# A hybrid state-space, Fourier and attention step: adaLN in column groups between the x tiles, and a state output whose coefficient step is cut into parts

## The chip, the core and the metric

The kernel runs on one core of one Trainium2 chip. The metric is the device time of one execution in microseconds (us). The median of three runs of the kernel before is 2755.11 us (2753.56 to 2757.28).

TensorE is called PE here, VectorE DVE, ScalarE ACT, GpSimd POOL; SP is the engine whose queue issues nearly all DMAs.

## What is computed

Two layers work on 128 context tokens (conditioned by `c_ctx`) and 1024 latent tokens (by `c`), 1024 channels each. Cut to what matters here:

```python
m = silu(cvec) @ ada_w + ada_b
shift, scale, gate = split(m)
h = rmsnorm(x, norm_g) * (1.0 + scale) + shift
a_in, a_gate, f_in, f_gate, q, k, v, c_gate = split(h @ w_in)
for d in (forward, backward):
    a_bar, b_bar = s5_discretise(a_re[d], a_im[d], log_dt[d], b_re[d], b_im[d])
    hs = s5_scan(u32, a_bar, b_bar, h0, rev)
    y = y + real(einsum(hs, c_mat))
    finals.append(hs[:, 0] if rev else hs[:, -1])
za = gelu(ya) @ glu_w
yf = fourier_mix(f_in) @ fnet_w
yc = attention(rope(rms(q)), rope(rms(k)), v)
x = x + gate * (merge of the three gated branches) @ w_out
```

The outputs are both token sets after a final RMS norm, the context keys and values, and the final state of each scan direction.

## The kernel before, in words

Tokens stand along the free axis: channels on the 128 partitions, 1152 token columns in three thirds (`j`) of 384. Large products are made of three passes: each fp32 operand is split into a rounded high part and a low part (`whi`, `wlo`, `hh`, `hl`), and `mm3` issues three matmuls per 128 x 128 block of weights. `dense(n)` runs the next n blocks from a list: for each third, 8 channel blocks k, into a `pd` accumulator (two buffers), which ACT then evacuates into `jo` and SP stores.

The program is written as Python generators that `drive` interleaves by given rates. A scheduler then fixes the order of each engine's instructions when the program is built: it takes them by the order in which they were written, as soon as its own estimate says that they are ready. On the chip each engine's order is fixed, and semaphores hold an instruction until its inputs are there.

The change touches three places.

**The head** (`setup`, `ada_gen`, `ada_row`, `x_gen`, `rb_first_gen`, `h_first_gen`, and `run` at the end). Nine tiles of x (128 tokens each, 512 KB) are loaded, transposed on PE (`x_gen`, 8 transposes a tile, half of each evacuated by ACT and half by DVE at L415), and their squares summed. `ada_gen` computes the first layer's shift and scale: 16 weight units of 512 KB (`aw`, four buffers), two products of 512 columns a unit with the four columns of `silc` or `sc4` as stationary operand. Eight of the first 16 halves, and others, are split into `awr` (ACT rounds, DVE or POOL subtracts). A finished part is copied (`adarow`) and turned by four small matmuls with `sel`. `h_unit` then makes `hh` and `hl` for one k and one third: a multiply on DVE (L149 or L461), ACT with the bias, a subtraction on DVE. All x tiles come first, then the adaLN units.

**The final states** (`scan_gen`, `finals`). The scan is 128 steps of four DVE instructions on the states `H` (the tile `A1`, `A` in the profile). The context states end in column 16 after the sixteenth step. `finals`, called where the scan's generator ends, copies that column on ACT (`ss_fin`), transposes it twice on PE and stores it.

**The state output** (`ssm_out_gen`), after the q, k, v work of each layer and beside six dense blocks. For each of eight steps of four groups, `coef` multiplies exponents and output weights (`CA`: DVE product, POOL product, DVE sum, for real and imaginary part) and copies them into `CK` (L758 to L760, DVE). `toeplitz` multiplies `CK` on PE in four column groups (`tile_position`), and its result goes through DRAM into `TT` and on ACT into `TP`. Two steps later, four groups g are put out: three DVE copies (L803 to L805) turn the states of g into `Hg` (two buffers), then three products on PE and a GELU on ACT into `Y`, which is stored after every second step.

Helpers: L127 is every SP transfer, L142 every ACT instruction, L145 `tensor_tensor`, L149 `scalar_tensor_tensor`, L168 every matmul and L173 every transpose.

Of the kernel before, what the change touches and what calls it, by code (L numbers as in the profile page):

```python
# [18 lines left out]
DEPTH = 2  # L19
# [66 lines left out]
PACE = (1, 1)  # L86
HELD = 2
# [14 lines left out]
class Program:  # L102
# [73 lines left out]
    def setup(self):  # L176
# [3 lines left out]
        self.load_x(0, 1)  # L180
        self.identr = self.sb("identr", [128, 128], R)
        nc.gpsimd.dma_start(self.identr, I["ident"])
# [3 lines left out]
        for i in range(4):  # L186
            nc.vector.tensor_copy(self.fold[32 * i:32 * i + 32], self.ident[32 * i:32 * i + 32, 32 * i:32 * i + 32])
        self.half9 = self.sb("half", [128, 9])
        nc.gpsimd.memset(self.half9, -0.5)
        self.half = self.half9[:, :8]  # L190
        vecs = [("c", I["c"][0], 8), ("c_ctx", I["c_ctx"], 8), ("norm_g", I["norm_g"], 16), ("ada_b", I["ada_b"], 48),
                ("merge_b", I["merge_b"], 48)]
        st = self.sb("fvst", [128, 128], pool=self.xp)
        off = 0
        self.fv = {}
        col = self.sb("fv", [128, 128])
        for nm, ap, k in vecs:
            self.dma(st[off:off + k], ap.rearrange("l (k p) -> (l k) p" if len(ap.shape) == 2 else "(k p) -> k p", p=128))
            n = k // DEPTH
            for l in range(1 if len(ap.shape) == 1 else DEPTH):  # L200
                self.fv[nm, l] = col[:, off + n * l:off + n * l + (n if len(ap.shape) == 2 else k)]
            off += k
        ps = self.pst("pv")
        self.tr(ps[:, :off], st[:off])
        self.act(col[:, :off], ps[:, :off])
        self.mods = {}
        self.sel = self.sb("sel", [4, 2])
        self.dma(self.sel, I["sel"])
        self.silc = self.sb("silc", [128, KD, 4])
        nc.gpsimd.memset(self.silc, 0.0)  # L210
        sc = self.silc[:, :, 0:2]
        self.act(sc[:, :, 0], self.fv["c_ctx", 0], AF.Silu)
        self.act(sc[:, :, 1], self.fv["c", 0], AF.Silu)
        self.sc4 = self.sb("sc4", [128, KD, 4], R)
        self.act(self.sc4[:, :, 0:2], sc)
        self.tt(self.sc4[:, :, 2:4], sc, self.sc4[:, :, 0:2].bitcast(F), OP.subtract)
# [6 lines left out]
        self.dma(self.dmask, I["dmask"])  # L223
# [82 lines left out]
    def ada_gen(self, l, pool, parts, bufs=3, first=False):  # L306
        self.ada_alloc(l)
        units = [(o, k) for o in parts for k in range(4)]
        ld = {}
        def load(i):  # L310
            ld[i] = self.ada_load(l, pool, bufs, *units[i])
        for i in range(bufs - 1):
            load(i)
        for i, (o, k) in enumerate(units):
            if i + bufs - 1 < len(units):
                load(i + bufs - 1)
            if i == 0:
                pa = self.ps.tile([128, 3, 512], F, name="pa", tag="pa", bufs=1)
            ps = pa[:, i // 4 % 3]
            st = ld.pop(i)  # L320
            for h in range(2):
                ends = (k == 0 and h == 0, k == 3 and h == 1)
                if first and (h == 0 or i >= 16):
                    self.mm(ps[0:4, :], self.silc[:, 2 * k + h], st[:, h], *ends)
                else:
                    w = self.sb("awr", [128, 2, 512], R, bufs=3 if first else 2, pool=pool)
                    self.act(w[:, 0], st[:, h])
                    self.tt(w[:, 1], st[:, h], w[:, 0].bitcast(F), OP.subtract, e=self.nc.gpsimd if first and i >= 7 else None)
                    self.mm(ps[0:4, :], self.sc4[:, 2 * k + h], w[:, 0], ends[0], False)
                    self.mm(ps[0:4, :], self.sc4[:, 2 * k + h], w[:, 1], False, ends[1])  # L330
                if h == 0:
                    if i > 3 and k == 0:
                        self.ada_row(l, units[i - 1][0], row)
                    yield 2 * 216
# [3 lines left out]
            if i + 1 == len(units):  # L338
                self.ada_row(l, o, row)
            yield 2 * 216  # L340

    def ada_row(self, l, o, row):
        pc = self.pst("pt")
        for b in range(4):
            self.mm(pc[:, 2 * b:2 * b + 2], row[:, 128 * b:128 * b + 128], self.sel)
        self.ada_out(l, o, pc)
# [133 lines left out]
    def rb_first_gen(self, xT, ssq):  # L480
        self.tt(ssq[:, 0], ssq[:, 0], ssq[:, 1], OP.add)
        r = self.rstd_cols(ssq[:, 0], 9)
        self.rb = [self.rstd_rows(r[:, 3 * j:3 * j + 3], 3) for j in range(3)]
        self.h_tiles()
        self.xr0 = self.sb("xr0", [128, KD, 384], pool=self.xp)
        for k in range(KD):
            self.tt(self.xr0[:, k], xT[:, k, 0:384], self.rb[0], OP.mult)
            yield 500

    def h_first_gen(self, xT, js, ks):  # L490
        for j in js:
            for k in ks:
                if j == 0:
                    self.h_unit(0, j, k, self.xr0[:, k], None, self.xr_tile())
                else:
                    self.h_unit(0, j, k, xT[:, k, 384 * j:384 * j + 384], self.rb[j], self.xr_tile())
                yield 500
# [208 lines left out]
    def scan_gen(self, l):  # L706
# [31 lines left out]
    def ssm_out_gen(self, l, a_d, y_d):  # L738
# [8 lines left out]
        ca, tp = {}, {}  # L747
        U = {}

        def coef(i):  # L750
            g0 = 4 * i
            CA = self.sb("ss_CA", [128, 2, 4, 16, 8], bufs=3, pool=self.gp)
            y = self.outer(Er, Cr, Ei, Cn, g0, CA[:, 0])
            self.tt(CA[:, 0], CA[:, 0], y, OP.add)
            y = self.outer(Er, Cn, Ei, Cr, g0, CA[:, 1])
            self.tt(CA[:, 1], CA[:, 1], y, OP.subtract)
            for r, C in ((0, Cr), (1, Cn)):
                nc.vector.tensor_copy(CK[0:64, r, :, 8:15], CA[0:64, r, :, :, 0:7].rearrange("p q c t -> p q t c"))  # L758
                nc.vector.tensor_copy(CK[64:128, r, :, 0:7], CA[64:128, r, :, :, 1:8].rearrange("p q c t -> p q t c"))  # L759
                nc.vector.tensor_copy(CK[:, r, :, 7], C[:, g0:g0 + 4])  # L760
            ca[i] = CA

        def toeplitz(i):
            g0 = 4 * i
            ps = self.pst("pt")
            Bf = S["B"].rearrange("p g r c -> p (g r c)")
            for r in range(2):
                for q in range(4):
                    c0 = (g0 + q) * 32 + 16 * r
# [13 lines left out]

        for x in range(10):
            if 1 <= x < 9:
                toeplitz(x - 1)
            if x < 8:
                if x % 2 == 0:
                    U[x // 2] = self.u_load(a_d, x // 2)
                coef(x)  # L790
            yield 2000 if x == 0 else 1200
            i = x - 2
            if i < 0:
                continue
            g0 = 4 * i
            if i % 2 == 0:
                Y = self.sb("ss_Y", [128, 8, 145], bufs=1, pool=self.gp)
            for q in range(4):
# [796 lines left out]
```

## Time and profile before

| what | us |
|---|---|
| median of three runs | 2755.11 |
| the profiled execution's own time | 2752.03 |
| its span | 2750.3 |
| PE busy (16092 matmuls) | 2627.0 |
| DVE busy | 1826.6 |
| ACT busy | 1143.5 |
| POOL busy | 683.4 |

The span is the time from the first to the last recorded instruction of one execution; the own time of that execution is 1.7 us longer. Busy time is the sum of an engine's instructions. A matmul's end is modelled, so a busy PE can still run at a lower clock: PEclk is the share of full speed that was granted, 1.00 for 2.4 GHz and 0.50 for 1.2 GHz. A wait is put down to the engine and line that released it.

### The profile page before, as it was taken

To read this page: it belongs to the slowest core of one execution; us is meant where nothing else is said; L and a number is where in the kernel's file an instruction comes from. 1 tells how busy PE (TensorE), PEld (TensorE's weight loads), DVE (VectorE), ACT (ScalarE), POOL (GpSimd) and SP (SyncE) were. 2 spreads that over 40 slices of the span, in tenths; PEclk is the share of its full clock that TensorE was granted. 3 is DMA by queue.
4 is the path that set the end of the run, shared out by engine and by line. 5 is a ranking of instruction groups with operands and counts; after the bars stand their busy time and mean duration, and the time that the engine had idled before them with its cause. 6 is when DMAs were issued, how large, how long until landed. Compare 5 with 4: busy or idle time off the path is not lost. (4 is left out here: it accounts for less than half of the span.)

```text
span 2750.3 us, 44553 instructions
## 1 busy us (share of the span) xinstructions
PE 2627.0 (96%) x16092; PEld 2509.0 (91%) x16092; DVE 1826.6 (66%) x3933; ACT 1143.5 (42%) x2676; POOL 683.4 (25%) x521
## 2 busy tenths in 40 slices
PE   7998999899999999999999899999999999999998
PEld 3898999799999999999989899989989998999998
DVE  6549955856558889866572797577654788891343
ACT  5461145331355565423345322543223655553244
POOL 3241122322321020132343212233222202102223
PEclk9999999999999999999999999999999999999999
DMA  6632223566263345544543222345645334433244
GB/s 223 178 99 84 95 87 110 150 191 207 86 202 114 110 138 153 173 126 114 165 146 93 95 89 84 107 125 160 211 154 174 109 121 150 143 121 98 80 121 149
DMA packets 459997, 366.85 MB, mean 133 GB/s; under 512 B 72953, under 2 KB 432001, under 8 KB 459777
## 3 DMA queue, kind: packets, MB, share of 16 engines
q1 hardware_dynamic: 458480, 359.75, 42.9%
q0 software_dynamic: 1296, 4.26, 0.5%
q8 instruction: 127, 2.08, 0.3%
q14 instruction: 94, 0.76, 0.1%
HBM read 243.52 MB, written 120.39 MB: 132 GB/s over the span
## 5 line engine op out<-in xcount | busy, mean ns | idle before, releaser
L168 PE MATMUL pd<-hh,whi 128*128 128x384 f32 x2496 | 857.1, 344 | 24.0 <-ACT jo L142 20.1
L168 PE MATMUL pd<-hh,wlo 128*128 128x384 f32 x2496 | 844.6, 339 | 3.2 <-POOL wlo L145 3.2
L168 PE MATMUL pd<-hl,whi 128*128 128x384 f32 x2496 | 843.1, 338 | 1.3 <-DVE hl L149 1.3
L145 POOL TENSOR_TENSOR wlo<-wst,whi 128x512 fp32r<-128x512 f32 x312 | 437.9, 1405 | 1525.8 <-ACT whi L142 1404.8
L168 PEld LDWEIGHTS pd<-hh,whi 128*128 128x128 f32 x2496 | 472.5, 189 | 35.0 <-ACT jo L142 22.8
L168 PEld LDWEIGHTS pd<-hh,wlo 128*128 128x128 f32 x2496 | 472.5, 189 | 7.8 <-POOL wlo L145 5.7
L168 PEld LDWEIGHTS pd<-hl,whi 128*128 128x128 f32 x2496 | 473.1, 190 | 3.8 <-DVE hl L149 2.3
L168 PE MATMUL pd<-A,whi 128*128 128x384 f32 x1728 | 458.2, 342 | 8.2 <-ACT jo L142 4.9
L168 PEld LDWEIGHTS pd<-A,whi 128*128 128x128 f32 x1728 | 311.2, 189 | 11.7 <-ACT jo L142 5.6
L142 ACT ACTIVATE whi<-wst 128x512 fp32r<-128x512 f32 x312 | 196.0, 630 | 278.5 <-PE pd L168 190.6
L168 PE MATMUL pd<-A,wlo 128*128 128x384 f32 x864 | 293.9, 340 | 0.0
L1078 DVE TENSOR_REDUCE at_mx<-pa 128x1 f32<-128x1152 f32 x128 | 173.3, 1354 | 16.1 <-PE pa L168 15.7
L168 PE MATMUL pa<-at_K,at_Q 128*128 128x384 f32 x768 | 167.2, 347 | 8.6 <-ACT at_P L142 5.8
L142 ACT ACTIVATE at_PT<-pt 128x384 fp32r<-128x384 f32 (+1 forms) x260 | 114.9, 490 | 144.0 <-PE pt L173 143.6
L142 ACT ACTIVATE at_P<-pa,at_mx 128x1152 f32<-128x1152 f32 x128 | 158.1, 1235 | 20.7 <-DVE at_mx L1078 19.4
L168 PEld LDWEIGHTS pd<-A,wlo 128*128 128x128 f32 x864 | 163.2, 189 | 0.1
L168 PEld LDWEIGHTS pa<-at_K,at_Q 128*128 128x128 f32 x768 | 128.3, 188 | 29.0 <-ACT at_P L142 25.5
L168 PE MATMUL pt<-qkW,hh 128*128 128x384 f32 x576 | 150.7, 343 | 0.0
L168 PE MATMUL pv<-at_PT,at_V 128*128 128x256 f32 x1152 | 148.8, 283 | 0.0
L168 PEld LDWEIGHTS pv<-at_PT,at_V 128*128 128x128 f32 x1152 | 144.7, 191 | 0.8
L142 ACT ACTIVATE jo<-pd 128x384 f32<-128x384 f32 x120 | 58.0, 485 | 198.1 <-PE pd L168 96.5
L145 DVE TENSOR_TENSOR at_PT<-pt,at_PT 128x384 fp32r<-128x384 f32 (+1 forms) x260 | 133.1, 550 | 10.0 <-ACT at_PT L142 7.8
(294 smaller groups left out, 3772.3 us busy)
## 6 DMA issues: line engine op xcount, KB each, us to landing
aw<-in_ada_w_dram SPq DMA_DIRECT2D x48, 512.0 KB, 4.8
wst<-in_merge_w_dram SPq DMA_DIRECT2D x96, 256.0 KB, 3.0
wst<-in_w_in_dram SPq DMA_DIRECT2D x80, 256.0 KB, 2.9
td<-jo SPq DMA_DIRECT2D x96, 192.0 KB, 2.3
jt<-td SPq DMA_DIRECT2D x96, 192.0 KB, 2.8
wst<-in_w_out_dram SPq DMA_DIRECT2D x64, 256.0 KB, 2.9
sgd<-jo SPq DMA_DIRECT2D x72, 192.0 KB, 2.0
jt<-sgd SPq DMA_DIRECT2D x64, 192.0 KB, 2.7
```

The lines of the kernel that those rows point to most:

```text
L142: return self.nc.scalar.activation(out, in_, func, **kw)
L145: return (e or self.nc.vector).tensor_tensor(out=out, in0=a, in1=b, op=op)
L168: return self.nc.tensor.matmul(out, w, x, start=first, stop=last, **kw)
L1078: nc.vector.tensor_reduce(out=mx[:, 0:1], in_=src, axis=AX.XY if m3 else AX.X, op=OP.max, negate=True)
```

## The change

In the head, the four parts of adaLN are computed in plain fp32, without `awr`. The conditioning columns stand in `silp`, padded with zeros to 32 columns, and the eight products of a part go to four groups of 32 columns of PE (`tile_position=(0, 32 * q)`); the sum over the groups is in the matmuls with `fold4`, which also turn the row. There are seven `aw` buffers in place of four. The parts stand between the x tiles: three tiles, part 2, a tile, part 0, two tiles, `h` of four k for two thirds, part 3, a tile, part 1, the rest. The RMS factors are made for each third by itself. Loads of x are spread between the `aw` loads; norm_g, ada_b, merge_b and dmask are loaded on POOL's queue; `sel` is no longer loaded.

`finals` is called after the q, k, v work, and its copy is on DVE, pinned behind DVE's instructions written before it.

In the state output, the coefficient step is a generator of four parts that alternate with the four groups put out. The `CK` copies are on ACT. `turned` makes `Hg` two groups ahead with three buffers (`HGB`).

```diff
-    def ada_gen(self, l, pool, parts, bufs=3, first=False):
+    def ada_first_gen(self, l, pool, parts):
...
+            if i % 4 == 3:
+                for t in ((3,), (4, 5), (6,), (7, 8))[i // 4]:
+                    self.load_x(t, t + 1)
...
             for h in range(2):
-                ends = (k == 0 and h == 0, k == 3 and h == 1)
-                if first and (h == 0 or i >= 16):
-                    self.mm(ps[0:4, :], self.silc[:, 2 * k + h], st[:, h], *ends)
-                else:
-                    w = self.sb("awr", [128, 2, 512], R, bufs=3 if first else 2, pool=pool)
-                    self.act(w[:, 0], st[:, h])
-                    self.tt(w[:, 1], st[:, h], w[:, 0].bitcast(F), OP.subtract, e=self.nc.gpsimd if first and i >= 7 else None)
-                    self.mm(ps[0:4, :], self.sc4[:, 2 * k + h], w[:, 0], ends[0], False)
-                    self.mm(ps[0:4, :], self.sc4[:, 2 * k + h], w[:, 1], False, ends[1])
...
+                q = 2 * (k % 2) + h
+                self.mm(ps[32 * q:32 * q + 32], self.silp[:, 2 * k + h], st[:, h], k < 2, k >= 2, tile_position=(0, 32 * q))
+            if i + bufs < len(units):
+                load(i + bufs)
             if k == 3:
-                row = self.sb("adarow", [4, 512], bufs=1, pool=pool)
-                self.act(row, ps[0:4, :])
...
+                row = self.sb("adarow", [128, 512], bufs=1, pool=pool)
+                self.act(row, ps)
+                pc = self.pst("pv")
+                for b in range(4):
+                    self.mm(pc[:, 2 * b:2 * b + 2], row[:, 128 * b:128 * b + 128], self.fold4)
...
+    def rb_first(self, ssq, j):
+        c = slice(3 * j, 3 * j + 3)
+        self.tt(ssq[:, 0, c], ssq[:, 0, c], ssq[:, 1, c], OP.add)
+        self.rb[j] = self.rstd_rows(self.rstd_cols(ssq[:, 0, c], 3), 3)
...
-        self.finals(l)
...
-        self.act(fin, H[:, :, :, 16])
+        self.tc.keep_in_program_order(self.nc.vector.tensor_copy(fin, H[:, :, :, 16]))
...
+        def coef_gen(i):
...
+            for r, (a, b, op) in enumerate(((Cr, Cn, OP.add), (Cn, Cr, OP.subtract))):
+                y = self.sb("ss_o2", [128, 4, 16, 8], bufs=1, pool=self.gp)
+                self.tt(CA[:, r], e4(Er), f4(a), OP.mult)
+                self.tt(y, e4(Ei), f4(b), OP.mult, e=nc.gpsimd)
+                self.act(CK[:, r, :, 7], a[:, g])
+                yield
+                self.tt(CA[:, r], CA[:, r], y, op)
+                self.act(CK[0:64, r, :, 8:15], CA[0:64, r, :, :, 0:7].rearrange("p q c t -> p q t c"))
+                self.act(CK[64:128, r, :, 0:7], CA[64:128, r, :, :, 1:8].rearrange("p q c t -> p q t c"))
+                if r == 0:
+                    yield
...
+        def turned(g):
+            t = self.sb("ss_Hg", [128, 2, 145], bufs=HGB, pool=self.gp)
...
+            cg = coef_gen(x) if x < 8 else iter(())
+            og = out_gen(x - 2) if x >= 2 else iter(())
             for q in range(4):
...
+                next(og, None)
+                next(cg, None)
+                yield (3 * 246 if x >= 2 else 500) + (600 if q == 0 else 0)
...
                     drive((q, 78), (self.dense(2), 21))
+                    self.finals(l)
...
+            self.run_some(xg, 6)
+            self.h_tiles((0,))
+            self.rb_first(ssq, 0)
+            for k in range(KD):
+                self.xr_first(xT, k)
             next(ada)
+            self.run_some(xg, 2)
+            next(ada)
+            self.run_some(xg, 4)
+            self.h_tiles((1,))
+            self.rb_first(ssq, 1)
+            for j in range(2):
+                for k in range(4):
+                    self.h_first(xT, j, k)
+            next(ada)
+            self.run_some(xg, 2)
+            next(ada)
+            for k in range(4, 8):
+                self.h_first(xT, 0, k)
+            self.run_all(xg)
+            self.run_all(ada)
+            self.h_tiles((2,))
+            self.rb_first(ssq, 2)
+            for k in range(4, 8):
+                self.h_first(xT, 1, k)
+            for k in range(KD):
+                self.h_first(xT, 2, k)
```

## Rows read from the trace of the kernel before

**Rows 1.** The page, busy time of PE to POOL over the span.

```profile
PE 2627.0 (96%) x16092; PEld 2509.0 (91%) x16092; DVE 1826.6 (66%) x3933; ACT 1143.5 (42%) x2676; POOL 683.4 (25%) x521
```

**Rows 2.** Timeline of ACT, first layer's scan: start, duration, instruction, idle before.

```profile
223.66 0.32 ACT L142 ACTIVATE ss_fin<-A 128x64 f32<-128x64 f32 x1 [12.25 <-DVE A L145]
```

**Rows 3.** Timeline of PE at the same place of both layers.

```profile
224.93 0.69 PE L168 MATMUL pd<-hh,whi 128*128 128x384 f32 x1 [7.84 <-ACT jo L142]
...
1566.74 0.69 PE L168 MATMUL pd<-hh,whi 128*128 128x384 f32 x1 [7.83 <-ACT jo L142]
```

**Rows 4.** Windows, first stall: PE, PEld, DVE, ACT, POOL, PEclk, DMA share, GB/s.

```profile
225.00:230.00 5.00, 5.00 (x16) 5.00 (x17) 4.72 (x18) 0.26 (x1) 0.85 (x1) 0.50 0.40 131
...
240.00:250.00 10.00, 10.00 (x60) 10.00 (x59) 9.45 (x35) 2.63 (x5) 2.13 (x2) 1.00 0.16 54
```

**Rows 5.** Timeline of PE in the head.

```profile
24.50 1.02 PE L168 MATMUL pa<-aw,silc 128*4 128x512 f32 x2
...
65.16 0.34 PE L168 MATMUL pd<-hh,whi 128*128 128x384 f32 x1
...
81.79 0.44 PE L168 MATMUL pd<-hl,whi 128*128 128x384 f32 x1 [0.60 <-DVE hl L149]
```

**Rows 6.** Windows over the head, columns as in group 4.

```profile
8.40:36.50 28.10, 24.02 (x112) 12.78 (x113) 14.51 (x41) 19.63 (x42) 2.13 (x1) 1.00 0.87 317
36.50:82.30 45.80, 37.52 (x144) 19.12 (x143) 39.99 (x76) 25.57 (x53) 21.31 (x13) 0.85 0.62 207
```

**Rows 7.** Windows of 2.5 us in the head, columns as in group 4.

```profile
12.50:15.00 2.50, 2.33 (x12) 1.93 (x11) 1.41 (x5) 2.47 (x8) 0.00 (x0) 1.00 1.03 419
...
35.00:37.50 2.50, 2.50 (x14) 1.17 (x14) 1.04 (x3) 1.39 (x3) 0.00 (x0) 1.00 0.74 235
```

**Rows 8.** Waits of the SP queue, 0 to 70 us: total us, times, longest.

```profile
SPq L127 <- PE pa L168: 15.5, 11, 2.1
```

**Rows 9.** Waits of PE, state output of the first layer, 480 to 560 us.

```profile
PE pt L168 <- issue: 3.4, 1, 3.4
PE pa L168 <- DVE ss_Hg L805: 2.3, 1, 2.3
PE pt L168 <- DVE ss_CK L760: 1.9, 2, 1.3
```

**Rows 10.** Waits of PE, state output of the second layer, 1820 to 1960 us.

```profile
PE pa L168 <- DVE ss_Hg L805: 3.3, 3, 1.7
PE pt L168 <- issue: 2.4, 1, 2.4
PE pd L168 <- ACT jo L142: 1.9, 1, 1.9
```

**Rows 11.** Window of 20 us in the state output, columns as in group 4.

```profile
480.00:500.00 20.00, 14.72 (x90) 11.06 (x89) 19.16 (x32) 6.52 (x15) 8.66 (x6) 0.83 0.62 171
```

**Rows 12.** Timeline of DVE behind the first layer's scan.

```profile
369.01 0.17 DVE L871 TENSOR_SCALAR qk_ss<-qk_ss 128x4 f32<-128x4 f32 x1 [10.85 <-ACT qk_j L142]
```

**Rows 13.** Timeline of PE at a Toeplitz step.

```profile
510.87 1.02 PE L168 MATMUL pt<-ss_CK,ss_B 128*32 128x240 f32 x16
511.82 0.44 PE L168 MATMUL pd<-hh,whi 128*128 128x384 f32 x1
```

**Rows 14.** Groups of instructions, 0 to 85 us: count, busy us, mean ns.

```profile
L149 DVE SCALAR_TENSOR_TENSOR xr<-A,modA,rb 128x384 f32<-128x384 f32 x16 | 12.6, 800 | 0.0
...
L145 DVE TENSOR_TENSOR xr<-A,rb 128x384 f32<-128x384 f32 x8 | 8.2, 1090 | 1.5 <-ACT rb L142 1.5
...
L145 DVE TENSOR_TENSOR awr<-aw,awr 128x512 fp32r<-128x512 f32 x7 | 4.6, 687 | 2.6 <-ACT awr L142 2.6
```

**Rows 15.** Instructions that read modA, 0 to 85 us: ns min/median/max.

```profile
L149 DVE SCALAR_TENSOR_TENSOR xr<-A,modA,rb x16: 604/608/1648, 49.0 to 79.6; 128x384 f32<-128x384 f32 x16
```

**Rows 16.** Instructions on ss_CK, whole span: ns min/median/max.

```profile
L758 DVE COPY ss_CK<-ss_CA x32: 549/1027/1490, 485.4 to 1912.7; 64x448 f32<-64x448 f32 x32
```

**Rows 17.** Instructions on ss_TP, whole span: ns min/median/max.

```profile
L142 ACT ACTIVATE ss_TP<-ss_TT x16: 1078/1104/1122, 504.8 to 1933.9; 128x512 f32<-128x512 f32 x16
```

More of the change, by code (lines that the diff above doesn't have):

```diff
@@ L86 @@
 PACE = (1, 1)
+HGB = 3
 HELD = 2
@@ L187, in setup @@
             nc.vector.tensor_copy(self.fold[32 * i:32 * i + 32], self.ident[32 * i:32 * i + 32, 32 * i:32 * i + 32])
+        self.fold4 = self.sb("fold4", [128, 2], pool=self.xp)
+        nc.vector.tensor_reduce(self.fold4, self.ident.rearrange("p (q c) -> p c q", c=32)[:, 0:2], axis=AX.X, op=OP.add)
         self.half9 = self.sb("half", [128, 9])
@@ L190, in setup @@
         self.half = self.half9[:, :8]
[L191 to L194, printed above, removed]
         self.fv = {}
[L196 to L202, printed above, removed]
@@ new lines, in setup @@
+        for i, vs in enumerate(vecs):
+            n = sum(k for _, _, k in vs)
+            st = self.sb(f"fvst{i}", [n, 128], pool=self.xp)
+            col = self.sb(f"fv{i}", [128, n])
+            off = 0
+            for nm, ap, k in vs:
+                (pdma if i else self.dma)(st[off:off + k], ap.rearrange("l (k p) -> (l k) p" if len(ap.shape) == 2 else "(k p) -> k p", p=128))
+                m = k // DEPTH
+                for l in range(1 if len(ap.shape) == 1 else DEPTH):
+                    self.fv[nm, l] = col[:, off + m * l:off + m * l + (m if len(ap.shape) == 2 else k)]
+                off += k
+            ps = self.pst("pv")
+            self.tr(ps[:, :n], st)
+            self.act(col, ps[:, :n])
+            if i == 0:
+                self.load_x(0, 3)
@@ L304, in ada_load @@
         return st
-    def ada_gen(self, l, pool, parts, bufs=3, first=False):
+    def ada_first_gen(self, l, pool, parts):
         self.ada_alloc(l)
         units = [(o, k) for o in parts for k in range(4)]
-        ld = {}
+        bufs, ld = 7, {}
         def load(i):
             ld[i] = self.ada_load(l, pool, bufs, *units[i])
-        for i in range(bufs - 1):
+            if i % 4 == 3:
+                for t in ((3,), (4, 5), (6,), (7, 8))[i // 4]:
+                    self.load_x(t, t + 1)
+        for i in range(bufs):
             load(i)
+        pa = self.ps.tile([128, 3, 512], F, name="pa", tag="pa", bufs=1)
         for i, (o, k) in enumerate(units):
[L315 to L318, printed above, removed]
             ps = pa[:, i // 4 % 3]
@@ L478, in h_gen, with xr_first, h_first @@
                 yield 900
[L480 to L497, printed above, removed]
+    def rb_first(self, ssq, j):
+        c = slice(3 * j, 3 * j + 3)
+        self.tt(ssq[:, 0, c], ssq[:, 0, c], ssq[:, 1, c], OP.add)
+        self.rb[j] = self.rstd_rows(self.rstd_cols(ssq[:, 0, c], 3), 3)
+    def xr_first(self, xT, k):
+        self.tt(self.xr0[:, k], xT[:, k, 0:384], self.rb[0], OP.mult)
+    def h_first(self, xT, j, k):
+        if j == 0:
+            self.h_unit(0, j, k, self.xr0[:, k], None, self.xr_tile())
+        else:
+            self.h_unit(0, j, k, xT[:, k, 384 * j:384 * j + 384], self.rb[j], self.xr_tile())
     def rhs_h(self, k, j):
```

135 lines of the change are left out of this document (54 added, 81 removed).

## The prediction, made before the changed kernel was run

> **What bounds the kernel now.** The page first [rows 1]: TensorE (PE) is busy 2627 of 2750 us, so only PE's idle time, some 123 us, and time at its lower clock can be won; work moved between other engines counts only where PE waits for it. I then took PE's waits one by one and looked at the three places that the diff touches.
>
> *The final states.* Inside the first layer's scan, ACT stands still for 12.25 us in front of one 0.32 us copy, `ss_fin<-A`, that waits for DVE [rows 2]: column 16 of the states is written by the sixteenth scan step, and ACT has the copy ahead of the evacuation of PE's accumulators. PE runs on for a while on its two `pd` buffers and then idles 7.84 us for `jo`, and 7.83 us at the same place of the second layer [rows 3]. It comes back at 0.50 of its clock, the 1.2 GHz level: 16 matmuls in 5 us against 60 in 10 later [rows 4], (30-16)/30*5 = 2.3 us more. So each layer pays about 10.2 us.
>
> *The head.* The first dense matmul starts at 65.16 us, but PE still waits for `hl` at 81.79 [rows 5]; that is a late piece of the last third of the first block, so the dense stage is in full flow only from about 82. What DVE does up to there: 14.5 us busy of the first 28.1, then 40.0 of 45.8 [rows 6]. DVE is the bound of the second half because the first was half empty: the adaLN units come late. Loads ran at 419 GB/s while x came in and at 235 around 35 us [rows 7], when the SP queue waited eleven times, 15.5 us in all, for PE to free a weight buffer [rows 8].
>
> *The state output.* PE waits in the stage around 480 to 560 us for the Toeplitz coefficients (3.4 and 1.9) and for the turned states (2.3) [rows 9]; in the second layer for turned states 3.3, Toeplitz 2.4 and smaller ones [rows 10]. In 480 to 500 us DVE is busy 19.16 of 20, ACT only 6.52, and the mean clock is 0.83 [rows 11].
>
> **The change, part by part.**
>
> *Final states: -20 us.* The copy goes from ACT to DVE, behind everything issued there before it, and the call moves from the end of the scan to the end of the q, k, v work. Nothing then holds ACT in the scan, so 2*10.2 = 20.4 us go. Does another thing catch PE 10 us later? Behind the scan DVE idles 10.85 us until ACT has evacuated the first `qkv` product [rows 12], so the scan is not what PE would meet next: that slack takes up the 10.2 us nearly whole. What is added: one DVE copy of about 0.3 us (ACT's 0.32), the same two transposes, two ACT copies and one store, now at the pool's end. Nothing queues behind a long wait, but the next pool's tiles in the same memory may start later by that chain. The nearest row for a step of it is the 0.32 us copy, so five short steps and a store are bounded by 0 and about 3 us a layer; I take 0.2, since six dense blocks are there to cover it. -20.
>
> *Head: -18 us.* Removed: seven DVE subtractions `awr`, 4.6 us, and nine on GpSimd; 16 ACT roundings; half the adaLN matmul forms. All 32 products are now plain fp32, two PE instructions each, 1.02 us a pair [rows 5]: 33 us if serial. They go to four column groups. The nearest row for that is the Toeplitz step: sixteen instructions of 240 columns in 1.02 us, next full matmul 0.95 us after their start [rows 13]; so groups overlap, and two at a time I cost the units at 16*1.02 = 16 us, spread over a head in which PE has room. Each switch of shape shows as 0.1 us there (0.44 for 0.34), times 32 is 3 us, off the path; I take 0.
>
> The Trainium skill, TensorEngine Tiling (Array Packing), Key Properties, says that changing the tiling mode, not just the tile, drains TensorE, and here x transposes at full width alternate with the groups. By that rule, were no overlap left, PE would have 16 us more to do in the head, and my term would shrink to about -8; the row above shows a cost of a tenth of a microsecond instead, so the trace does not bear out the dear reading.
>
> Loads: x and 16 adaLN units are 25 transfers of 512 KB, 13.1 MB. At 419 GB/s that is 31 us, at 235 it is 56 [rows 7]. Buffers go from four to seven and PE frees them without a rounding chain in between, so I take near the upper rate: last unit at about 40 us. DVE: 54.5 us of work [rows 6] less 4.6 for `awr`; 16 products `xr` took 0.80 us in the mean for 0.608 in the median, 3.1 us, and eight others took 1.09 for 384 columns where `awr` took 0.687 for 512, so at least 3.2 [rows 14, 15]; GpSimd ran its subtractions beside them and has none now. About 43.5 us are left; they start when the first x tile lands, at 8.4 us now (where the first window begins [rows 6]), hence 52 us if DVE never waits. Three rms chains (GpSimd power, transposes, ACT) and four adaLN rows come in between: an estimate of 10 us of waiting, of the 19 us there now [rows 6]. So the last `hl` is ready at about 62 instead of 82: -20, and PE, which idles more just before, starts a few microseconds at its lower clock: +2.3 as after the stalls above. -18. Ends: -24 (few waits) and -8 (loads at 235 GB/s: 56 us and then the last 12 pieces of `h`, about 1.2 us each, to 72, plus 2). What is moved: x loads of the SP queue now stand between adaLN loads, five small loads go to the GpSimd queue (nothing there waits but the first power), three short powers replace one; all lie beside the loads of the first 10 us.
>
> *State output: -14 us.* Listed idle time is 3.4+2.3+1.9 in the first layer and 3.3+2.4 in the second, with small ones some 8 us each; the clock adds about (1-0.83)*20 = 3.4 us, part of it idle anyway, say 2. That is 20 us for both layers, and 5 more in waits at the end of the stage and the start of the next [rows 10]. The coefficient step's four copies leave DVE (about 1.03 us each for half of them [rows 16]), so some 25 us a layer go to ACT. ACT's nearest row is the permuted copy of 512 columns, 1.104 us [rows 17]: for 448 columns at most that, four a step, eight steps: 35 us a layer on an engine idle two thirds of the stage; costed at nothing, as long as ACT does not wait itself. Turned states are made two groups ahead with a third buffer, which takes away DVE's 2.3 and 3.3. Of the Toeplitz waits I keep half: the chain multiply, GpSimd, add, copy stays as long, only more dense work stands in front of its first use. So -14, between 0 and -24, with a loss bounded in the rivals.
>
> Sum: -20-18-14 = -52. Against the profiled execution (2752.03; its span 2750.3) that gives 2700; its time is 3 below the median of 2755.1, so **2703**.
>
> **Rivals.**
> 1. *The head stays bound by loads* (four waits for a buffer in PE's order): -8 instead of -18, 2713. For it: today's 235 GB/s. Against: 419 with the same transfers when nothing held them. 0.13.
> 2. *State output gains nothing*: PE's order is fixed when the program is built, and each Toeplitz step may again be placed before its coefficients. 2717. For it: the 3.4 us wait at such a place. 0.14.
> 3. *The final states' stall only moves*: PE's transposes or the next pool wait for the pinned copy. If half comes back, 2713. Against: DVE has slack behind the scan [rows 12]. 0.08.
> 4. *Slower: ACT's queue in the state output.* Each of 32 half steps puts two copies on ACT that wait for a DVE add, which waits for GpSimd; a `jo` evacuation queued behind them stops PE as in rows 2 and 3. PE covered 12.25-7.84 = 4.4 us there, so it decides from waits of over 4.4 us. The end is slower if all cost over (20+18)/32 = 1.2 us beyond that; at 1.6 each, 51 us, the time is 2768. Against: GpSimd's product is part of a 5 us chain already. 0.05.
> 5. *Column groups do not overlap* (the drain, told above): 2713. 0.06.
>
> **Numbers.** The main case has 0.54, own range 2690 to 2716. The rivals on the gaining side reach 2717, two of them together about 2727; below, head and state output both at their ends give 2687. Range 2687 to 2730. A measurement can tell about 0.2%, 5.5 us, from no change; only the fourth rival, or all the others together, gets there: faster 0.92, same 0.03, slower 0.05.
>
> **What would show it.** No ACT wait of 12 us in the scan, no 7.8 us PE wait, and a scan that ends at the same distance from its start. Last PE wait for `hl` near 62 us, adaLN loads over by 42, no `awr`. PE's waits for `ss_Hg` gone, for `ss_CK` halved, now put down to ACT. I am wrong if the scan's 10 us come back as a PE wait in the q, k, v stage, if the last `hl` is later than 72 us, or if PE's waits for `jo` grow in the state output.

## The result, and the profile after

The changed kernel takes **2717.83 us** (median of four runs, 2706.61 to 2720.30), against 2755.34 (median of four, 2753.56 to 2757.28): a ratio of 0.986, with a 95% interval of 0.984 to 0.988. The forecast was 2703, its range 2687 to 2730. The profiled execution took 2717.28 us with a span of 2715.5, 34.8 less than before, where the sum had -52.

The first part of the page, answering to [rows 1]:

```profile
span 2715.5 us, 44526 instructions
PE 2604.6 (96%) x16093; PEld 2504.5 (92%) x16093; DVE 1762.0 (65%) x3837; ACT 1201.1 (44%) x2754; POOL 669.1 (25%) x518
```

PE's busy time fell by 22.4 us and its idle time by 12.4. Busy time can fall although nearly the same matmuls run, because fewer of them run at the lower clock; that returns below. DVE lost 65 us, ACT gained 58: work moved between engines that do not set the end.

**A ruler.** To see where the 34.8 us came from, I counted the matmuls into `pd` (10,086 records in either trace). The n-th is the same piece of dense work in both, so its start is a clock on the work. Between two counts, the difference says what a stage gained:

| stage (n of the `pd` matmul) | before, us | after, us | gained |
|---|---|---|---|
| head (start to 288, four dense blocks) | 0 to 123.3 | 0 to 114.8 | 8.4 |
| first scan's stall (648 to 720) | 212.8 to 236.0 | 204.2 to 216.7 | 10.7 |
| first state output (1584 to 2376) | 474.5 to 668.9 | 454.8 to 644.5 | 4.7 |
| second scan's stall (5688 to 5760) | 1554.6 to 1577.6 | 1526.9 to 1539.3 | 10.5 |
| second state output (6624 to 7344) | 1816.6 to 1996.9 | 1777.6 to 1956.6 | 1.4 |
| everything else, to n = 10080 (4.6 gained between these stages, 5.7 lost behind the last) | | | -1.1 |

**The scan.** The windows of the first scan, answering to [rows 4] at the same place of the work (columns: window, its length, PE, PEld, DVE, ACT, POOL busy with instructions, granted clock, DMA share, GB/s):

```profile
215.00:220.00 5.00, 5.00 (x30) 5.00 (x30) 4.86 (x11) 1.36 (x3) 2.76 (x2) 1.00 0.29 92
220.00:225.00 5.00, 5.00 (x31) 5.00 (x30) 4.66 (x22) 0.49 (x1) 0.00 (x0) 1.00 0.29 92
```

No gap and no 0.50 behind it; the 7.84 and 7.83 us of [rows 3] are gone. The copy is now on DVE, some 240 us later in the first layer, and takes less than ACT's 0.32:

```profile
L716 DVE COPY ss_fin<-A x2: 205/207/209, 463.1 to 1785.5; 128x64 f32<-128x64 f32 x2
```

**The head.** PE's own sequence (columns: start, us, instructions, and in brackets the idle time before and its releaser), answering to [rows 5]:

```profile
10.62 0.48 PE L174 MATMUL pt<-ident,hl 128*128 128x128 f32 x1 [7.23 <-DMA hl<-in_x_prompt_dram]
...
24.63 1.92 PE L169 MATMUL pa<-aw,silp 128*32 128x512 f32 x16
...
42.45 3.63 PE L169 MATMUL pa<-aw,silp 128*32 128x512 f32 x16
46.86 1.05 PE L169 MATMUL pv<-fold,adarow 128*128 128x2 f32 x8 [0.79 <-ACT adarow L143]
...
51.70 1.97 PE L174 MATMUL pt<-ident,hl 128*128 128x128 f32 x8 [2.85 <-ACT A L143]
54.22 0.69 PE L169 MATMUL pd<-hh,whi 128*128 128x384 f32 x1 [0.55 <-ACT whi L143]
...
72.62 0.44 PE L169 MATMUL pd<-hl,whi 128*128 128x384 f32 x1 [0.64 <-DVE hl L150]
```

Read three things. Sixteen instructions of 512 columns run in 1.92 us: eight products at 0.24 us each, where one took 1.02 before [rows 5]. The last adaLN part is turned at 46.86, and the last x tile is transposed at 51.70, after it. The first dense matmul starts 11 us earlier (54.22 for 65.16), and the last wait for `hl` is at 72.62 instead of 81.79.

The windows show what the loads did, and what DVE did up to that last `hl`; the last two answer to [rows 6]:

```profile
5.00:10.00 5.00, 0.00 (x0) 0.00 (x0) 0.00 (x0) 0.00 (x0) 0.00 (x0) 1.00 1.04 178
30.00:35.00 5.00, 3.01 (x20) 1.47 (x24) 4.16 (x14) 4.11 (x12) 1.01 (x1) 1.00 1.04 397
40.00:45.00 5.00, 5.00 (x24) 2.72 (x27) 3.18 (x12) 0.90 (x3) 0.00 (x0) 0.50 1.12 337
45.00:50.00 5.00, 3.06 (x24) 1.75 (x16) 1.58 (x7) 2.44 (x7) 0.00 (x0) 0.84 0.17 26
10.60:48.00 37.40, 28.40 (x161) 16.27 (x162) 22.91 (x72) 20.01 (x43) 1.89 (x2) 0.91 0.98 348
48.00:72.60 24.60, 19.02 (x89) 17.55 (x87) 22.12 (x43) 15.82 (x33) 6.63 (x5) 0.72 0.46 169
```

The transfers are over by 45, and the DMA share is near or above 1 up to there. DVE has 14.5 us idle of the first 37.4 and is then busy 22.1 of 24.6. PE runs at 0.50 in 40 to 45 and at 0.72 in the mean of 48 to 72.6. What DVE waited for between its first x tile and 73 us (its four longest totals; 1.6 us more in two single waits):

```profile
DVE mod L146 <- PE pv L169: 6.4, 3, 3.8
DVE A L407 <- PE pt L174: 4.2, 5, 1.9
DVE hl L150 <- ACT hh L143: 2.3, 5, 0.6
DVE xr L146 <- ACT rb L143: 2.2, 1, 2.2
```

**The state output.** PE's waits in the first layer, over the whole stage of the ruler (455 to 645), answering to [rows 9]:

```profile
PE pd L169 <- ACT jo L143: 2.2, 1, 2.2
PE pa L169 <- ACT ss_TP L143: 2.0, 2, 1.8
PE pt L169 <- ACT ss_CK L143: 1.6, 2, 0.9
PE pd L169 <- DVE jo L150: 1.6, 3, 0.8
PE pt L169 <- issue: 1.3, 1, 1.3
PE pv L174 <- DVE ss_fin L716: 1.2, 1, 1.2
PE pd L169 <- POOL wlo L146: 1.1, 1, 1.1
```

[Rows 9] stop at 560 us. Over the whole stage before (474 to 669) they become these, with the Toeplitz waits as they were:

```profile
PE pa L168 <- DVE ss_Hg L805: 3.1, 2, 2.3
PE pd L168 <- ACT jo L142: 3.0, 1, 3.0
PE pd L168 <- DVE jo L149: 1.6, 2, 0.9
PE pa L168 <- ACT ss_TP L142: 1.0, 1, 1.0
```

In the second layer after (1777 to 1957), answering to [rows 10], and then two lines of the whole stage before (1816 to 1997) that stand beside those:

```profile
PE pd L169 <- ACT jo L143: 3.2, 2, 2.9
PE pd L169 <- DVE jo L150: 2.4, 4, 0.9
PE pa L169 <- ACT ss_TP L143: 2.2, 2, 1.4
PE pt L169 <- ACT ss_CK L143: 1.6, 2, 0.9
PE pt L169 <- issue: 1.3, 1, 1.3
```

```profile
PE pd L168 <- DVE jo L149: 1.6, 2, 0.9
PE pa L168 <- ACT ss_TP L142: 0.6, 1, 0.6
```

The turned states (`ss_Hg`) are gone from both lists, and the Toeplitz waits (issue and `ss_CK`) fell from 3.4 + 1.9 to 1.3 + 1.6 in the first layer. What stands there instead is mostly put down to ACT: `ss_TP`, `ss_CK`, `jo`. The waits for `jo`, ACT's and DVE's together, went from 4.6 to 3.8 in the first layer and from 3.5 to 5.6 in the second. The start of the stage (answering to [rows 11]) and both state outputs whole, between the counts of the ruler, after and then before:

```profile
475.00:495.00 20.00, 16.24 (x116) 13.48 (x117) 12.34 (x26) 17.54 (x30) 7.74 (x7) 1.00 0.45 142
454.80:644.50 189.70, 178.28 (x1151) 167.06 (x1149) 107.93 (x221) 96.35 (x182) 53.17 (x38) 0.99 0.60 178
1777.60:1956.60 179.00, 166.15 (x1071) 154.35 (x1070) 105.15 (x214) 93.34 (x176) 47.81 (x36) 0.99 0.60 179
```

```profile
474.50:668.90 194.40, 180.20 (x1150) 168.78 (x1148) 138.17 (x268) 62.08 (x132) 52.31 (x38) 0.97 0.59 174
1816.60:1996.90 180.30, 167.85 (x1068) 156.76 (x1067) 134.14 (x261) 59.25 (x126) 50.00 (x36) 0.97 0.61 177
```

Subtract busy from length: PE idles 11.4 and 12.9 us now, 14.2 and 12.4 before. So idle time gave only 2.4 us of the 6; the other 3.6 are busy time, at 0.99 of the clock for 0.97. In the second layer the idle time did not shrink at all: other waits took its place.

### The profile page after: what moved, and what is told of

Same layout as the page of the kernel before. It is cut to its first block, busy times and chain, and to the rows that moved or that the text cites. A ratio compares the mean times of both kernels' runs of the same rounds, so it can differ in the third digit from the quotient of the medians.

```text
span 2715.5 us, 44526 instructions
## 1 busy us (share of the span) xinstructions
PE 2604.6 (96%) x16093; PEld 2504.5 (92%) x16093; DVE 1762.0 (65%) x3837; ACT 1201.1 (44%) x2754; POOL 669.1 (25%) x518
```

## The experiments

Each was run once beside one run of the kernel before on the same chip. A stage of the ruler repeats to 2 or 3 us among kernels that do not differ there (the first state output: 2.7 to 4.9 in the change, e5, e6 and e10; the head: 7.0 to 9.2 in the change, e2, e7, e8, e9, e11 and e12, and 10.7 in `e3_head`, which has the same head), so small differences of one stage are not read. Totals are read with care: in eleven of the twelve (not in `e9_act_no_pin`) PE waits 1.5 to 3.1 us for a small product of the second layer's adaLN, whose code none of them touches, where the change does not wait, and by the ruler they lose 2 to 5 us against the change around that place.

| kernel | us (before beside it) | head | scan 1 | output 1 | scan 2 | output 2 |
|---|---|---|---|---|---|---|
| the change | 2717.83 (2755.34) | 8.4 | 10.7 | 4.7 | 10.5 | 1.4 |
| e1_finals | 2742.36 (2753.24) | 0.1 | 10.7 | -5.0 | 10.5 | -6.2 |
| e3_head | 2742.27 (2753.24) | 10.7 | 1.0 | 0.0 | -0.1 | -0.4 |
| e4_out | 2747.68 (2753.24) | -0.2 | 1.0 | 4.4 | -0.3 | 2.7 |
| e2_pin_at_scan | 2745.86 (2753.24) | 7.9 | 10.7, then -12.4 | 4.2 | 10.5, then -12.3 | 2.9 |
| e9_act_no_pin | 2738.61 (2757.47) | 8.1 | 0.9 | 2.6 | -0.3 | 3.9 |
| e5_x_loads_first | 2724.79 (2751.92) | 2.5 | 10.7 | 4.8 | 10.5 | 2.5 |
| e6_x_before_part3 | 2723.15 (2751.92) | 1.8 | 10.7 | 4.9 | 10.5 | 0.9 |
| e10_x_before_part1 | 2721.35 (2757.47) | 8.3 | 10.7 | 2.7 | 10.5 | 2.4 |
| e7_own_tiles | 2723.48 (2751.92) | 7.0 | 10.7 | 4.1 | 10.5 | -0.4 |
| e8_ck_half_dve | 2718.52 (2751.92) | 9.2 | 10.7 | 2.7 | 10.5 | 2.0 |
| e11_hgb2 | 2719.41 (2756.94) | 8.2 | 10.7 | 4.1 | 10.5 | 0.6 |
| e12_ck_all_dve | 2728.51 (2756.94) | 8.6 | 10.7 | -3.9 | 10.5 | -0.6 |

### One part alone

The kernel before with one part of the change each: the final states, the head, the state output.

```diff
# e1_finals
-        self.finals(l)
...
-        self.act(fin, H[:, :, :, 16])
+        self.tc.keep_in_program_order(self.nc.vector.tensor_copy(fin, H[:, :, :, 16]))
...
                     drive((q, 78), (self.dense(2), 21))
+                    self.finals(l)
# e3_head
-    def ada_gen(self, l, pool, parts, bufs=3, first=False):
+    def ada_first_gen(self, l, pool, parts):
...
# e4_out
+HGB = 3
...
-        def coef(i):
...
+        def coef_gen(i):
...
```

> The kernel before with the final states' part of the change alone (copy on DVE, pinned, called after the q, k, v work). Theory: the two stalls of 7.8 us and the lower clock behind them go, 10.7 us in the first layer and 10.5 in the second as between the two kernels' matmul times, and the time falls by 21 us less what the new place costs: the state output starts 3 us later, since its tiles wait for the store of the final states, so 15 to 21 us in all, 2734 to 2740. Rival: the gain belongs to the whole change and some of the 10 us comes back as a wait in the q, k, v work: less than 12 us.

> The kernel before with the head's part alone. Theory: the head gives 8.4 us by the first dense blocks, as between the two kernels, and nothing behind it depends on it: 2747. The last wait of PE for hl near 72.6 us. Rival: the head's gain is partly the other parts' (by the order that the scheduler finds): less than 5 or over 12 us.

> The kernel before with the state output's part alone. Theory: its own gain is larger than the 5.2 and 1.8 us that stand between the two kernels at these stages, because there the final states' store holds its start by 3 us; alone 7 to 10 us in the first layer and 4 to 7 in the second, 2738 to 2745. Rival: ACT, busy 17.5 of 20 us at the start of the stage with copies of 1.07 us, is what limits it; then it gives 5 and 2 us alone too, about 2748.

The stalls of the scan are worth 10.7 and 10.5 us whatever else is in the kernel. But `e1_finals` ends only 9.7 us earlier by the ruler's last count: its state outputs, in which no line differs from the kernel before, lose 5.0 and 6.2. Its waits of PE over the whole span, and the start of its first state output:

```profile
PE pa L168 <- DVE ss_Hg L804: 11.5, 8, 2.3
```

```profile
475.00:495.00 20.00, 14.59 (x93) 11.47 (x92) 18.78 (x30) 5.80 (x13) 11.00 (x8) 0.91 0.67 177
```

PE waits 11.5 us for turned states, against 3.1 and 3.3 in the two stages before, and DVE is full (18.78 of 20), as it was before [rows 11]. So the old state output gives back half of what the scan won; the new one, with DVE at 12.34, does not. `e1_finals` was expected to gain 15 to 21 us and gained 10.9, by neither of its theories: nothing came back in the q, k, v work. `e3_head` gained 10.7 in the head where 8.4 were expected. `e4_out` came out at its rival's figure. By the ruler the three parts alone sum to 9.7 + 9.6 + 4.3 = 23.6, together to 34.6. Of the 11 us between, the two state outputs make 10.6 (-0.6 and -3.9 summed over the single parts, 4.7 and 1.4 together); the other stages differ by up to 4 us either way, the small product named above among them, and cancel. Against `e1_finals`, with the final states moved in both, the new state output is worth 9.7 and 7.6 us.

What makes the old one lose when it starts earlier was not isolated, but the trace shows a part of it: it starts later by the ruler. DVE's first coefficient product begins 11.7 us behind the stage's first count in `e1_finals` (8.0 before), and its last turned state 129.1 us behind it (123.5 before). DVE idles just ahead of that product, behind the copy of the final states:

```profile
475.34 0.69 DVE L145 TENSOR_TENSOR ss_CA<-ss_EC,ss_Cre 128x512 f32<-128x512 f32 x1 [3.03 <-issue]
```

The changed kernel starts as late (11.6) and does not lose; whether the old stage would still lose with an early start was not run.

### The final states: place and pin

In the changed kernel, the pinned copy back at the scan's end, or the copy at the new place but on ACT and not pinned:

```diff
# e2_pin_at_scan
             yield 800
+        self.finals(l)
...
-                    self.finals(l)
# e9_act_no_pin
-        self.tc.keep_in_program_order(self.nc.vector.tensor_copy(fin, H[:, :, :, 16]))
+        self.act(fin, H[:, :, :, 16])
```

> The changed kernel with the call of the final states put back to the end of the scan, the copy still pinned on DVE. Theory: what matters for the scan is the pin and the engine, not the place, so no stall returns; and the wait of 3.07 us of DVE and of 6.6 us of POOL for the store of the final states at the start of the state output goes, by which PE's waits there shrink by 2 to 3 us a layer: 2711 to 2714. Rival: dense blocks cover that start anyway, and the time stays within 1 us a layer of the changed kernel's.

> The changed kernel with the copy of the final states on ACT again and not pinned; its call stays at the new place, behind the q, k, v work. Theory: a call written later does not move the copy, since the scheduler issues what it takes to be ready as soon as ACT is free by its estimate; so ACT waits again for the sixteenth scan step, both stalls of some 10.5 us return, and the time is 2736 to 2741. Rival: the place is what counts and the pin is not needed: 2715 to 2721.

`e9_act_no_pin` came out as expected, `e2_pin_at_scan` at neither figure. With the pin at the scan's end, ACT no longer stalls in the scan, but PE does behind it: its two transposes are placed ahead of dense work and wait for a copy that stands behind the whole scan on DVE. PE's waits of the whole span:

```profile
PE pv L174 <- DVE ss_fin L717: 21.2, 2, 10.6
```

That is the third rival (the stall only moves), in full, and it cost more than the stall. Without the pin, the copy floats back by itself: written after the q, k, v work, it stands in ACT's order in the middle of the scan (the tile's instructions, with the idle time before them):

```profile
L143 ACT ACTIVATE ss_fin<-A x2: 320/320/320, 215.6 to 1551.5; 128x64 f32<-128x64 f32 x2
...
  DVE A L146: 24.5, 2
```

ACT waits 24.5 us in two pieces and PE again 7.8 us at a time for `jo`. So neither half of the edit does it alone: not the pin without the place (`e2_pin_at_scan`), and not the place without the pinned DVE copy (`e9_act_no_pin`, which changes engine and pin at once; which of these two it needs was not told apart). The place at which a line is written is not where it runs.

### The head: x earlier

Three attempts to let the x tiles, and with them DVE's work on `h`, come sooner:

```diff
# e5_x_loads_first
-            if i % 4 == 3:
-                for t in ((3,), (4, 5), (6,), (7, 8))[i // 4]:
-                    self.load_x(t, t + 1)
+            if i == 3:
+                self.load_x(3, 9)
# e6_x_before_part3: the same, and in run
-            next(ada)
-            self.run_some(xg, 2)
-            next(ada)
...
             self.run_all(xg)
-            self.run_all(ada)
             self.h_tiles((2,))
             self.rb_first(ssq, 2)
+            next(ada)
...
+            next(ada)
+            for j in range(3):
+                for k in range(4, 8):
+                    self.h_first(xT, j, k)
+            self.run_all(ada)
# e10_x_before_part1
-                for t in ((3,), (4, 5), (6,), (7, 8))[i // 4]:
+                for t in ((3,), (4, 5), (6, 7, 8), ())[i // 4]:
...
             next(ada)
-            self.run_some(xg, 2)
-            next(ada)
...
             self.run_all(xg)
-            self.run_all(ada)
             self.h_tiles((2,))
             self.rb_first(ssq, 2)
...
+            next(ada)
...
+            self.run_all(ada)
```

> The changed kernel with the x tiles 3 to 8 loaded right behind the fourth adaLN unit, all ahead of the units that wait for a buffer. Theory: the head ends late because tiles 7 and 8 are loaded last (issued at 36 us), so the last third's rms chain and its h come after the last adaLN part; loaded early they are transposed in waits of PE, and the last wait for hl falls from 72.6 us to about 66: 3 to 7 us in all. Rival: the loads of 5 to 45 us run at 370 to 397 GB/s already, the adaLN units become later by what x becomes earlier, and PE's order still has tiles 7 and 8 behind the last part: within 2 us of the changed kernel.

> As the run before, and all nine x tiles and the last rms chain stand ahead of the third adaLN part, with four k of the last third's h between the parts. Theory: then only eight h pieces of four k each wait for the last part; DVE's idle 20 us between 10 and 50 us are used, and the last wait for hl falls to 62 to 66 us: 6 to 10 us less than the changed kernel. Rival: the last adaLN part, now later, sets the end: less than 3 us.

> The changed kernel with x tiles 7 and 8 loaded and worked ahead of the fourth adaLN part only (all x in front of the third had let the adaLN buffers run dry), with the last rms chain and four k of the last third's h there too. Theory: what holds the head's end is DVE's work behind the last adaLN part, 24.6 us from 48 to 72.6; with nine to ten of it moved ahead the last wait for hl falls to about 66, though the last part comes 2 to 3 us later: 4 to 7 us less than the changed kernel at the first dense blocks. Rival: whatever x gains is lost by the later adaLN units, as in the two runs with early x: no gain or a loss.

All x loads early is a loss: the head gains 2.5 and 1.8 instead of 8.4. The transfers run dry while adaLN is still to come, and its last part is turned at 55.28 for 46.86 (the window, then PE's sequence, of `e5_x_loads_first`):

```profile
30.00:40.00 10.00, 8.35 (x38) 5.57 (x42) 3.58 (x13) 4.25 (x9) 1.80 (x2) 0.63 0.43 159
```

```profile
55.28 1.05 PE L169 MATMUL pv<-fold,adarow 128*128 128x2 f32 x8 [0.78 <-ACT adarow L143]
```

A share of 0.43 where the change has 1.04 at 30 to 35. Both runs missed their theory; the first also lost more than its rival allowed. I read it so that the seven `aw` buffers stand full while PE takes x tiles first, and no adaLN load can follow; that chain was not tested by itself. With only the last part behind the x tiles (`e10_x_before_part1`) the first two dense blocks were 2.7 us ahead of the change (11.2 gained at n = 144 for 8.5; but `e3_head`, with the change's own order, has 10.8 there), and after four blocks nothing was left, as its rival said:

```profile
89.63 0.33 PE L174 MATMUL pv<-ident,ss_c 128*128 128x128 f32 x1 [2.58 <-ACT ss_Cre L143]
```

The preparation of the state space is what PE meets next: it waits 2.58 us for it where the change waits 1.4, and the granted clock of 90 to 95 us is then 0.66 for 1.00. None of the three shortened the head.

### The state output: ACT, DVE, buffers

```diff
# e7_own_tiles
-        fin = self.sb("ss_fin", [128, 2, 32], pool=self.gp)
+        ft = self.sb("jt", [128, 384], bufs=3)
+        fin = ft[:, 256:320].rearrange("p (r g) -> p r g", r=2)
...
-        o = self.sb("qk_sq", [32, 2, 64, 2], pool=self.gp)
+        o = ft[0:32, 0:256].rearrange("p (d n r) -> p d n r", d=2, n=64)
# e8_ck_half_dve
-                self.act(CK[64:128, r, :, 0:7], CA[64:128, r, :, :, 1:8].rearrange("p q c t -> p q t c"))
+                nc.vector.tensor_copy(CK[64:128, r, :, 0:7], CA[64:128, r, :, :, 1:8].rearrange("p q c t -> p q t c"))
# e11_hgb2
-HGB = 3
+HGB = 2
# e12_ck_all_dve: e8's edit on all three copies into CK
```

> The changed kernel with the final states held in a tile that lives on through both stages, so that the state output does not wait for their store. Theory: the 3.07 us wait of DVE and 6.6 us of POOL at the start of the state output go, PE's first waits for the coefficients shrink: 1 to 4 us a layer. Rival: dense blocks cover the start, and the waits for the coefficients come from the order in which PE has the Toeplitz products, placed by an estimate: under 1 us a layer.

> The changed kernel with one of the two large coefficient copies of each half step back on DVE. Theory: ACT takes 1.07 us for such a copy against 0.55 to 1.03 on DVE and is busy 17.5 of 20 us at the start of the state output, so the chain to the Toeplitz product is shorter by a microsecond a half step and PE's waits for ss_CK and ss_TP (some 5 us a layer) halve: 2 to 3 us a layer less. Rival: these waits follow PE's fixed order and move with it: within 1 us a layer, or slower since DVE's copies again collide with POOL's products.

> The changed kernel with two buffers for the turned states, so one group ahead instead of two. Theory: the waits for turned states (11.5 us in both layers when the final states alone are moved) are gone because the coefficient step stands in parts between the groups, so that DVE's copies of a group never queue behind a whole step; the second group ahead adds little, and PE waits at most 2 us a layer for ss_Hg. Rival: the third buffer is what took them away; they return with 4 to 6 us a layer.

> The changed kernel with all coefficient copies back on DVE; parts and turned states stay. Theory: DVE is then as full at the start of the stage as before the change (19 of 20 us) and the late start behind the final states' store costs it as with the final states alone: the stage gives 3 to 6 us less a layer. Rival: cutting the step into parts is what counts; a copy takes DVE 0.55 to 1.03 us where ACT takes 1.07, so PE's waits for ss_CK do not grow and the stage stays within 1.5 us a layer.

`e7_own_tiles` takes the final states' store out of the pool, because in the change the first coefficient product on DVE waits 3.07 us for that store:

```profile
466.43 0.69 DVE L146 TENSOR_TENSOR ss_CA<-ss_EC,ss_Cre 128x512 f32<-128x512 f32 x1 [3.07 <-DMA out_dram<-qk_sq]
```

The wait went, and by the ruler the first product begins 8.7 us behind the stage's first count for 11.6, but the stage did not get shorter (4.1 for 4.7, -0.4 for 1.4): as the rival said, this wait does not set its length. All copies back on DVE (`e12_ck_all_dve`) costs 8.6 us in the first layer and 2.0 in the second, where 3 to 6 a layer were expected; the first 20 us look like before the change again, DVE full and the clock at 0.81:

```profile
475.00:495.00 20.00, 17.12 (x100) 14.35 (x99) 19.30 (x44) 6.50 (x12) 6.83 (x5) 0.81 0.42 125
```

So in the first layer the copies on ACT carry what this part gains; the 2.0 of the second are within what the ruler repeats to. They are not free there: each takes 1.066 us, 64 of them 68 us (the tile's instructions in the change), ACT is busy 17.54 of 20 us at the stage's start, and PE's waits for `ss_CK` and `ss_TP` are put down to ACT.

```profile
L143 ACT ACTIVATE ss_CK<-ss_CA x64: 1005/1066/1112, 469.4 to 1869.2; 64x448 f32<-64x448 f32 x64
```

That a full ACT is what makes them is not shown: half of the copies on each engine (`e8_ck_half_dve`) brings ACT down to 10.85 of the same 20 us (DVE 16.76, granted clock 0.83), PE then waits 3.7 us a layer for `ss_CK` by DVE, and the stages gain 2.7 and 2.0 for 4.7 and 1.4: no difference that this ruler shows, where 2 to 3 us a layer were expected. The third `Hg` buffer (`e11_hgb2`) is worth little: with two, one wait of 0.8 us for turned states comes back in either layer, and the stages gain 4.1 and 0.6, as expected. With the copies off DVE, turning one group ahead is nearly enough.

No version was found that clearly beats the change; `e8_ck_half_dve` (2718.52) and `e11_hgb2` (2719.41) stand within its own runs.

## Why the prediction was right or wrong

The sign and the range held; the sum was 17 us too hopeful, by the ruler: 1.2 more in the scan, 9.6 less in the head, 7.9 less in the state output, 1.1 lost elsewhere. This last is a net of 4.6 gained and 5.7 lost in stages that the prediction did not name.

**Final states: right.** -20 forecast, 21.2 measured. The two terms (idle time and lower clock) are both in the windows. The slack behind the scan took up the shift, as argued from [rows 12]: DVE's longest wait for `qk_j` in the q, k, v work fell from 10.8 to 2.9 us, and by the ruler nothing was lost between the scan and the state output. What the prediction had no price for is that this alone would have gained half, since the state output behind it pays; the change has both, and so the third rival is seen only in the variants.

**Head: right in mechanism, mis-sized.** -18 forecast, 8.4 measured. The step that failed is "an estimate of 10 us of waiting" with "they start at 8.4" and "43.5 us are left". By the windows the same sum reads: start at 10.6, 22.9 + 22.1 = 45.0 us of DVE work, and 14.5 + 2.5 = 17.0 us of idle time up to 72.6. So the work was right within 1.5 us, the start 2.2 late and the waiting 7 us longer, 10.7 in all. DVE's waits say which: for the adaLN rows (6.4) and the rms chains (2.2 and one of 0.9) they are 9.5, as estimated. What the sum left out are 4.2 us for x tiles not yet transposed (3.4 of them for the first three tiles, between 12 and 18 us), 2.3 between the two DVE steps of `h`, and 0.7. Loads as a whole went on to 45 us, at up to 397 GB/s rather than 419 and with only 178 in 5 to 10 us. The clock term was forecast at 2.3. The first dense matmul starts 10.9 us earlier and the stage gains 8.4; of the 2.5 between, 1.4 are busy time (57.0 us for the four blocks against 55.6, at 0.93 of the clock for 1.00) and the rest idle time. The forecast's own bound for a wrong step, an `hl` later than 72, was just crossed. The 8.4 is also the first rival's price and the forecast's own lower end, but not by their condition: loads did not run at 235 GB/s.

**Column groups: better than costed.** I took two at a time, 16 us for the 32 products. [Rows 13] said four already: at the 1.02 us that two instructions of 512 columns take [rows 5], sixteen of 240 would need 3.8 us one after another, and they took 0.95. Four run beside each other here too: 0.24 us a product, and 64 instructions with 11.9 us of PE time in the whole head, the last part's 3.63 at the lower clock included:

```profile
L169 PE MATMUL pa<-aw,silp 128*32 128x512 f32 x64 | 11.9, 722 | 0.0
```

The fifth rival falls. The Trainium skill, TensorEngine Tiling (Array Packing), Key Properties, says that a change of tiling mode drains TensorE and that tiles run in parallel; the second is plain in this row, and of the first the trace shows no idle time in front of these 64 instructions, though ends of matmuls are modelled and a short drain could hide in them. It paid nothing more: PE is busy 28.40 of the 37.40 us up to 48 and was not the head's bound.

**State output: mis-sized, near the second rival.** -14 forecast, 6.1 measured. What was to go went: the waits for `ss_Hg`, nearly half of the Toeplitz waits, and the lower clock, whose 2 us a layer came as 3.6 us of busy time in both. The step that failed is to count those waits as time won. They were 5.5 us less in the first layer's list, but idle time fell by only 2.8 there and rose by 0.4 in the second: waits for `ss_TP`, `ss_fin` and `wlo` took their place in the first, for `jo` and `ss_TP` above all in the second. "Costed at nothing, as long as ACT does not wait itself" is the nearest the forecast came to this; the copies took 1.066 us, as bounded from [rows 17], and come densely at the stage's start. Whether ACT or PE's fixed order sets the new waits stays open: with half of the copies off ACT the stage was no shorter, and with all of them off it (`e12_ck_all_dve`) it was longer. The fourth rival, a net loss through ACT's queue, did not come. But the forecast's own sign of being wrong, "if PE's waits for `jo` grow in the state output", came in the second layer, by 2.1 us.

**Chances.** The likeliest case, 0.54, did not come in full: 2717.83 lies just above its own 2716. Head and state output both came near the prices of the first two rivals, which the text put at about 2727 together and counted into the range, but the head not by the first rival's mechanism.

## What to carry to other kernels

Where a stage starts half empty, count what its engine can do only after the last input has landed; the sum of its work says little, and the order of the loads is the lever and the risk at once. An instruction that waits long in a fixed order must be moved together with its dependants and held there: moved alone, the wait reappears at the next engine, and unpinned it floats back. Test parts of a change in pairs, since a stall removed upstream can be paid back by a stage downstream, as here by 11 of 21 us.

## What the runs showed that was not expected

The DMA engines were counted as fully busy (1.04) in 5 to 10 us while they moved 178 GB/s; later the same share moved 397. The packets were not smaller: those of 4096 bytes took 379 ns in the mean there and 163 ns in 30 to 35. What slowed them was not tried.

PE ran at 0.50 of its clock through 40 to 45 us although it was busy all of that window, after stretches in which it had been busy 3.01 and 2.50 of 5 us (30 to 35 and 35 to 40). The sixteen column-group instructions of the last part took 3.63 us there; in `e3_head`, with the same head, they ran at 1.00 and took 1.92, and its head gained 10.7.

Behind the second state output, where no line differs from the kernel before, the change loses 5.7 us; `e3_head` gains 0.3 there and the other variants lose 1.2 to 5.0. Two stretches hold it (n = 7344 to 8352 and 9792 to 10080): PE is busy 4.0 us longer in them, at a granted clock of 0.99 and 0.97 for 1.00 in both, and idle 1.8 longer. What sets this off was not tried.

The four changed runs spread over 2706.61 to 2720.30, the four of before over less than 4 us.

A product far from any edit became a wait in eleven of the twelve variants. In `e8_ck_half_dve` it waits where neither the kernel before nor the change does, which is a reason to compare stages and not totals:

```profile
1149.00 0.25 PE L169 MATMUL pt<-aR,fold 128*32 128x8 f32 x8 [3.15 <-issue]
```
